# A planner's costs: VectorE and GpSimd use SBUF by turns, ScalarE loads tables, GpSimd's results arrive later

## The chip, the cores and the metric

The kernel runs on one core of a Trainium2 chip. The metric is the device time of one execution in microseconds (us). The engines are named as in the profile: PE (TensorE's products; PEld are its weight loads), DVE (VectorE), ACT (ScalarE), POOL (GpSimd) and SP (SyncE, which here only issues transfers).

## The reference

One layer of a hybrid encoder block on 512 rows of width 1024, in float32. Three sub-layers, each with an RMS norm before and after and a residual sum:

```python
h = rms_norm(x, g_mix_pre)
q_f, k_f, v_f, f_logit, q_c, k_c, v_c = split(h @ w_in)          # 8 + 8 heads of 64
o_f = fox_attention(q_f, k_f, v_f, log_sigmoid(f_logit + b))     # causal, bias c_t - c_s
o_c = chunked_rel_attention(q_c, k_c, v_c, rel_bias)             # chunks of 64, learned bias
mix = concat(rms_norm(o_f), rms_norm(o_c)) @ w_out
x = x + rms_norm(mix, g_mix_post)
x = x + rms_norm(memory_cross_attention(rms_norm(x), rms_norm(mem), w_q, w_kv, w_o))  # 4 heads, 256 tokens
x = x + rms_norm((silu(h @ w_gate) * (h @ w_up)) @ w_down)       # h = rms_norm(x), width 2816
```

## The kernel before

**Products in halves.** Every float32 operand of a large product is split into a rounded half `hi` and a rest `lo`, and the product is made as three PE products: hi by hi, hi by lo and lo by hi (`mm3`, L410, L411, L413). So each block of weights that a transfer brings (`raw`) costs one cast on ACT (`hi`, L392) and one subtraction on DVE (`lo`, L393). That is most of what DVE does.

**Stages.** The first 250 us or so hold the token mixer: four groups of four heads (`order`, first two groups of the forgetting attention, then two of the chunked one). For each group, value, query and key projections (`group_proj`), then the heads. A head (`head`, L787 to L833) walks over four row blocks i = 0 to 3: scores on PE (L796, L797, tile `ps_s`, two banks), sum with the bias and row maximum on DVE (L800, tiles `p_i` and `nm`), exponential on ACT (L810), reciprocal and scaling on DVE (L811, L812), transposes on PE (L815, tile `ps_t`), and the split of the transposed block into `pth` (ACT, L817) and `ptl` (DVE, L818). Then the product with the values (L824, `ps_o`), and ACT and DVE gather the output `o` (L832, L833). After every two heads, `pair_out` writes `oh` (ACT, L836) and `ol` (DVE, L837), and GpSimd squares the output (L843, `o`) and adds it up (L845, `sq`). These sums reach PE in `group_rs` (L851). GpSimd also masks the diagonal block of each bias (L767), adds squares of the memory tokens (L888, `msq`) and raises small tiles to a power for the norms (L418).

The out projection, the memory's keys and values, the queries and the cross-attention follow (softmax rows `xp`, L1067 to L1079; their transposes are split into `pt`, L1085, L1086; products with `vm` into `ps_o`). At the end of the cross-attention a Silu on one column (L1100) makes ACT load the other table of functions ahead of its use. From about 430 us on, the feed-forward stage runs; its order is written out by hand.

**The planner.** Everything up to there is emitted in program order and then put in order by `planned_order` (L90 to L291). It goes through the instructions as a list scheduler: for each engine it keeps the time at which it is free, takes the engine whose next start is earliest, and gives it the ready instruction that comes first in the program (PE prefers to keep its narrow transposes together). `duration` estimates how long an instruction takes; `reached` adds what a result needs to get to another engine (`SIGNAL`, or `TO_PE` for PE); buffers and PSUM banks must be free in its own account (`may_start`). The order so found is then fixed on each engine, PE, DVE, ACT, POOL and SP's queue of transfers alike. So its times don't run the chip; they only decide what stands in front of what.

Of the kernel before, what the change touches and what calls it, by code (L numbers as in the profile page):

```python
# [10 lines left out]
AF = mybir.ActivationFunctionType  # L11
# [24 lines left out]
ENGINES = mybir.EngineType  # L36
MATMUL, NARROW, TURNED, SUMMED, GATHER, ISSUE = 0.4424, 108.0, 12.0, 100.0, 1500.0, 440.0
TAIL = {ENGINES.DVE: 84.0, ENGINES.Activation: 104.0, ENGINES.Pool: 55.0}
SIGNAL = {
    (ENGINES.Activation, ENGINES.DVE): 32.0, (ENGINES.DVE, ENGINES.Activation): 35.0,  # L40
    (ENGINES.PE, ENGINES.Activation): 37.0, (ENGINES.PE, ENGINES.DVE): 37.0,
    (ENGINES.DVE, ENGINES.Pool): 80.0, (ENGINES.Activation, ENGINES.Pool): 67.0,
    (ENGINES.Pool, ENGINES.DVE): 36.0, (ENGINES.Pool, ENGINES.Activation): 34.0,
}
TO_PE, LANDED = 350.0, 60.0


def number(dims):
    n = 1
    for d in dims:  # L50
        n *= d[1]
    return n
# [37 lines left out]
def planned_order(tc, instructions, homes):  # L90


    def tile_of(pattern):
        ap = getattr(pattern, "bass_ap", None)
        return ap.tensor.name if ap is not None and ap.tensor.name in homes.tiles else None

    def in_psum(pattern):
        return homes.tiles[tile_of(pattern)][0] == "ps"
# [24 lines left out]
    def outline(x):  # L123
        return x[:3] + ([(min(a for a, _ in x[3]), max(b for _, b in x[3]))],)

    def duration(i):
        kind = type(i).__name__
        n = number(list(i.outs[0].bass_ap.ap)[1:])
        read = [number(list(a.bass_ap.ap)[1:]) for a in i.ins if tile_of(a)]
        columns = sum(n > 8 and m == 1 for m in read)  # L130
        if i.engine == ENGINES.PE:
            return MATMUL * n + 2.0 if n > P else NARROW
        if i.engine == ENGINES.Activation:
            return (284.0 if len(i.outs) > 1 else 160.0) + 0.838 * n + 80.0 * columns
        if i.engine == ENGINES.Pool:
            if n <= 8:
                return 174.0 if kind == "InstTensorCopy" else 1450.0 if n == 1 else 1040.0
            if kind == "InstTensorTensor" and tile_of(i.ins[0]) != tile_of(i.ins[1]):
                return 25.0 + 4.1 * n
            return 25.0 + (0.96 if kind == "InstMemset" else 2.0) * n  # L140
        if kind == "InstCustomDveAnt":
            return 245.0 + 0.99 * n
        if kind == "InstTensorReduce":
            return 158.0 + 1.02 * read[0]
        if kind == "InstMemset":
            return 70.0 + 0.8 * n
        if kind == "InstReciprocal" or n < 8:
            return 158.0
        full = [a for a in i.ins if tile_of(a) and number(list(a.bass_ap.ap)[1:]) > 8]
        if len(full) < 2 and not any(map(in_psum, full)):  # L150
            return 213.0 + 0.526 * n
        return 150.0 + 1.046 * n + 60.0 * columns

    def halves(i):
        starts = []
        for a in [i.outs[0]] + list(i.ins):
            ap = getattr(a, "bass_ap", None)
            if ap is not None and ap.ap[0][1] >= 8:
                whole = number([(0, n) for n in list(ap.tensor.shape)[1:]]) if tile_of(a) else 0
                starts.append(ap.offset // whole if whole else 0)  # L160
        return (starts + starts + [0, 0])[:2]

    nodes = [i for i in instructions if type(i).__name__ not in ("BassTilePoolBoundary", "InstRegisterMove")]
    written, read, touched, uses, guests, previous, last_of = {}, {}, {}, {}, {}, {}, {}
    after, missing, used = [{} for _ in nodes], [0] * len(nodes), []
    for k, i in enumerate(nodes):
# [14 lines left out]
        for n, x in enumerate(ins + outs):  # L181
            x, writes = outline(x), n >= len(ins) or homes.tiles[x[0]][0] == "ps"
# [19 lines left out]
    for line in after:  # L202
        for k in line:
            missing[k] += 1

    ready, at = {}, [0.0] * len(nodes)
    for k, i in enumerate(nodes):
        if not missing[k]:
            ready.setdefault(i.engine, []).append(k)
    free, ends, place, landed, order, lasts, room = {}, {}, {}, {}, {}, {}, {}  # L210

    def reached(e, other, transfer):
        if e == other and not transfer:
            return 20.0 if e == ENGINES.PE else -20.0
        return TO_PE if other == ENGINES.PE else LANDED if transfer else SIGNAL.get((e, other), 40.0)

    def may_start(k):
        t = at[k]
        for name in used[k]:
            if name in lasts:  # L220
                continue
            if previous[name] and previous[name] not in lasts:
                return None
            key = homes.tiles[name]
            if not room.setdefault(key, [None] * homes.bufs[key]):
                return None
            guest = room[key][0]
            for other in [guest] if guest else [n for n in uses if homes.tiles[n] in homes.under(key)]:
                if uses[other]:
                    return None  # L230
                for (e, transfer), end in lasts[other].items():
                    t = max(t, end + reached(e, nodes[k].engine, transfer))
        return t

    patience = [GATHER if {x for x in names if x in homes.patient} else 0.0 for names in used]
    narrow, after_narrow = [i.engine == ENGINES.PE and duration(i) <= NARROW for i in nodes], False
    while any(ready.values()):
        best = None
        for e, waiting in ready.items():
            starts = [(t, k) for t, k in ((may_start(k), k) for k in waiting) if t is not None]  # L240
            if not starts:
                continue
            now = max(free.get(e, 0.0), min(starts)[0])
            able = [(k, t) for t, k in starts if t <= now + 1.0]
            if e == ENGINES.PE:
                alike = [x for x in able if narrow[x[0]] == after_narrow and (after_narrow or x[1] <= now)]
                late = [x for x in able if narrow[x[0]] and x[1] + patience[x[0]] <= now]
                able = alike if after_narrow and alike else late or alike or able
            if best is None or (now, str(e)) < best[:2]:
                best = now, str(e), e, *min(able)  # L250
        _, _, e, k, t = best
        ready[e].remove(k)
        i, start = nodes[k], max(free.get(e, 0.0), t)
        transfer = type(i).__name__ == "InstDMACopy"
        if transfer:
            free[e] = start + ISSUE
            end = landed[e] = max(start + 1900.0, landed.get(e, 0.0)) + 4 * number(i.outs[0].bass_ap.ap) / 300.0
            if e == ENGINES.Pool:
                end += 1500.0
        elif e == ENGINES.PE:  # L260
            cost = duration(i) + (0.0 if narrow[k] or not after_narrow else SUMMED if summed else TURNED)
            after_narrow, summed = narrow[k], number(list(i.outs[0].bass_ap.ap)[1:]) <= 8
            waited = t > free.get(e, 0.0) + 5.0 and cost > 100.0
            free[e] = start + cost + (95.0 if waited else 0.0)
            end = start + max(cost, 60.0) + 170.0
        else:
            if halves(i) != place.get(e, [0, 0]):
                start = max(start, ends.get(e, 0.0) + 28.0)
            place[e] = halves(i)
            end = ends[e] = start + duration(i)  # L270
            free[e] = max(start + 20.0, end - TAIL[e])
        order.setdefault(e, []).append(i)
        for name in used[k]:
            if name not in lasts:
                lasts[name] = {}
                room[homes.tiles[name]].pop(0)
            lasts[name][e, transfer] = end
            uses[name] -= 1
            if not uses[name]:
                room[homes.tiles[name]].append(name)  # L280
        for j, in_turn in after[k].items():
            other = nodes[j].engine
            at[j] = max(at[j], start if in_turn else (start if e == other == ENGINES.PE else end) + reached(e, other, transfer))
            missing[j] -= 1
            if not missing[j]:
                ready.setdefault(other, []).append(j)
# [15 lines left out]
def hybrid_block_kernel(  # L302
# [628 lines left out]
    with tc.tile_pool(name="cross", bufs=1, reuse_waits="tile") as cp:  # L931
# [508 lines left out]
        class Seven:  # L1440
# [55 lines left out]
        eight(2, gate_eight, IN_STEP)  # L1496
        planned = list(nc.cur_bb.bb.instructions)
        lasts = planned_order(tc, planned, homes)
        own_order = tc.manual_schedule(
            engines={mybir.EngineType.PE, mybir.EngineType.DVE, mybir.EngineType.Activation}  # L1500
# [316 lines left out]
```

## Time and profile before

| | us |
|---|---|
| median of 3 runs (757.09 to 757.48) | 757.11 |
| the profiled execution, whole | 757.56 |
| its span, first to last instruction | 755.8 |
| busy: PE / DVE / ACT / POOL | 744.0 / 603.1 / 445.3 / 59.3 |
| mean granted clock of PE | 0.998 of full |

The profile tells for each instruction its start and length, for each idle stretch what ended it, and from that the chain of waits. Times in it are counted from the start of the span. PE's products are pipelined and their records overlap, so the distance between two starts says more on PE than busy time.

### The profile page before, as it was taken

What the parts mean: (1) busy time and instruction counts of PE and PEld (TensorE: products, weight loads), DVE (VectorE), ACT (ScalarE), POOL (GpSimd) and SP (SyncE); (2) the same over time, 40 slices, a digit from 0 to 9 for tenths busy, and PEclk for the clock granted to TensorE, in tenths of its full rate; (3) what the DMA queues carried; (4) which work ended last, traced back from release to release, by engine and by line L of the source; (5) the groups of instructions that cost most, each with busy time, mean ns of one, the idle gap of its engine ahead of it and who ended that gap; (6) DMA issues with size and microseconds to landing.
All of it is one profiled execution on the core that took longest, in us unless ns stands there. A gap on an engine that the chain in (4) does not pass through costs nothing.

```text
span 755.8 us, 12990 instructions
## 1 busy us (share of the span) xinstructions
PE 744.0 (98%) x5032; PEld 679.8 (90%) x5032; DVE 603.1 (80%) x1101; ACT 445.3 (59%) x817; POOL 59.3 (8%) x101
## 2 busy tenths in 40 slices
PE   9999999999999999999999999999999999999996
PEld 9988887898789988888878999999999999999995
DVE  8669999798788688445654698999989999998756
ACT  8569998686776458344554445666555557544321
POOL 1001232102201211000001200000000000000001
PEclk9999999999999999999999999999999999999999
DMA  7623233324214725411440023333333322243223
GB/s 254 168 81 97 73 88 112 112 71 144 67 57 138 277 75 181 137 57 56 142 145 21 29 97 105 110 110 112 113 112 112 112 85 84 84 139 113 85 84 111
DMA packets 62204, 82.16 MB, mean 109 GB/s; under 512 B 2872, under 2 KB 44344, under 8 KB 62144
## 3 DMA queue, kind: packets, MB, share of 16 engines
q1 hardware_dynamic: 60432, 76.34, 31.8%
q0 software_dynamic: 1280, 4.72, 1.8%
q8 instruction: 39, 0.64, 0.3%
q10 hardware_dynamic: 432, 0.29, 0.1%
q14 instruction: 21, 0.17, 0.1%
HBM read 79.22 MB, written 2.11 MB: 108 GB/s over the span
## 4 chain that ended last, share of the span: by engine, by line
PE 89%; ACT 5%; DVE 3%; issue 1%; DMA 1%; POOL 0%; POOLq 0%; DVEq 0%; ACTq 0%
PE ps_a L410 13%; PE ps_a L411 13%; PE ps_a L413 13%; PE ps_t L1400 3%; PE ps_t L1397 3%; PE ps_t L1398 3%; PE ps_s L1398 3%; PE ps_s L1400 3%; PE ps_s L1397 3%; PE ps_s L410 3%; PE ps_s L413 3%; PE ps_s L411 3%; PE ps_o L824 2%; PE ps_t L815 2%; PE ps_a L1400 1%; PE ps_a L1397 1%
## 5 line engine op out<-in xcount | busy, mean ns | idle before, releaser
L393 DVE TENSOR_TENSOR lo<-raw,hi 128x1024 fp32r<-128x1024 f32 x56 | 69.9, 1258 | 21.1 <-ACT hi L392 13.8
L413 PE MATMUL ps_a<-hTh,lo 128*128 128x512 f32 x192 | 76.2, 397 | 0.0
L411 PE MATMUL ps_a<-hTl,hi 128*128 128x512 f32 x192 | 76.2, 397 | 0.0
L410 PE MATMUL ps_a<-hTh,hi 128*128 128x512 f32 x192 | 75.8, 395 | 0.0
L392 ACT CAST hi<-raw 128x1024 fp32r<-128x1024 f32 x56 | 57.5, 1047 | 30.3 <-PE ps_a L411 20.4
L1193 DVE TENSOR_TENSOR ring_lo<-sums,ring_hi 128x1024 fp32r<-128x1024 f32 (+1 forms) x39 | 46.6, 1195 | 11.8 <-ACT ring_hi L1192 7.2
L1192 ACT CAST ring_hi<-sums 128x1024 fp32r<-128x1024 f32 (+1 forms) x39 | 40.2, 1030 | 16.5 <-PE ps_s L1398 16.5
L1192 ACT CAST ring_hi<-fraw 128x1024 fp32r<-128x1024 f32 (+1 forms) x26 | 26.5, 1032 | 33.6 <-DVE fraw L1279 17.5
L810 ACT ACTIVATE p<-p,nm 128x128 f32<-128x128 f32 (+1 forms) x64 | 36.0, 562 | 11.1 <-DVE nm L800 10.4
L413 PEld LDWEIGHTS ps_a<-hTh,lo 128*128 128x128 f32 x192 | 36.1, 188 | 6.5
L411 PEld LDWEIGHTS ps_a<-hTl,hi 128*128 128x128 f32 x192 | 36.1, 188 | 6.2
L410 PEld LDWEIGHTS ps_a<-hTh,hi 128*128 128x128 f32 x192 | 36.2, 188 | 6.2
L1193 DVE TENSOR_TENSOR ring_lo<-fraw,ring_hi 128x1024 fp32r<-128x1024 f32 (+1 forms) x26 | 30.9, 1199 | 11.3 <-ACT ring_hi L1192 11.3
L818 DVE TENSOR_TENSOR ptl<-ps_t,pth 128x128 fp32r<-128x128 f32 (+1 forms) x64 | 30.4, 483 | 1.7 <-ACT pth L817 1.5
L817 ACT CAST pth<-ps_t 128x128 fp32r<-128x128 f32 (+1 forms) x64 | 26.7, 420 | 8.3 <-PE ps_t L815 7.7
L815 PE MATMUL ps_t<-ident,p 128*128 128x128 f32 x160 | 28.1, 273 | 2.0 <-DVE p L812 2.0
L812 DVE TENSOR_SCALAR p<-p,rc 128x128 f32<-128x128 f32 (+1 forms) x64 | 28.3, 442 | 0.1
L1398 PE MATMUL ps_a<-b,ring_hi 128*128 128x256 f32 x92 | 25.5, 277 | 0.0
L815 PEld LDWEIGHTS ps_t<-ident,p 128*128 128x128 f32 x160 | 19.8, 140 | 6.4 <-issue 1.7
L1397 PE MATMUL ps_a<-b,ring_hi 128*128 128x256 f32 x92 | 25.5, 277 | 0.0
L1400 PE MATMUL ps_a<-b,ring_lo 128*128 128x256 f32 (+1 forms) x93 | 25.5, 276 | 0.0
L410 PE MATMUL ps_a<-hi,oh 128*128 128x512 f32 x64 | 25.3, 396 | 0.0
(572 smaller groups left out, 2774.6 us busy)
## 6 DMA issues: line engine op xcount, KB each, us to landing
raw<-in_dram SPq DMA_DIRECT2D x64, 512.0 KB, 3.7
fraw<-in_dram SPq DMA_DIRECT2D x26, 512.0 KB, 3.5
place<-in_dram SPq DMA_DIRECT2D x21, 512.0 KB, 4.3
more_room<-in_dram SPq DMA_DIRECT2D x15, 512.0 KB, 4.0
row<-gate_rows SPq DMA_DIRECT2D x8, 256.0 KB, 3.2
cb<-in_dram SPq DMA_DIRECT2D x8, 256.0 KB, 2.6
xo<-in_dram POOLq DMA_DIRECT2D x4, 512.0 KB, 7.5
rawv<-in_dram SPq DMA_DIRECT2D x3, 520.0 KB, 6.3
```

The lines of the kernel that those rows point to most:

```text
L392: act.copy(hi[:, j : j + n, :], raw)
L393: dve.tensor_tensor(out=lo[:, j : j + n, :], in0=raw, in1=f32(hi[:, j : j + n, :]), op=ALU.subtract)
L410: pe.matmul(dst, sh, mh, start=first, stop=False)
L411: pe.matmul(dst, sh, ml, start=False, stop=False)
L413: pe.matmul(dst[:, to], sl, mh[:, to], start=False, stop=last)
L810: act.activation(p[:, :n], p[:, :n], AF.Exp, bias=nm, scale=-1.0, accum_out=sm)
L815: pe.transpose(tp[:, k * P : (k + 1) * P], p[:, k * P : (k + 1) * P], ident)
L1192: act.copy(h2, v)
L1193: dve.tensor_tensor(out=l2, in0=v, in1=f32(h2), op=ALU.subtract)
L1397: pe.matmul(dst, w[0][:, k, :], b[:, 0, k, :], start=first and k == 0, stop=False, skip_group_check=more)
L1398: pe.matmul(dst, w[0][:, k, :], b[:, 1, k, :], start=False, stop=False, skip_group_check=more)
L1400: pe.matmul(dst[:, to], w[1][:, k, :], b[:, 0, k, to], start=False, stop=last and k == 3, skip_group_check=more,)
```

## The change

Three things in the planner's account, and nothing else in the kernel:

- DVE and GpSimd instructions of at least 64 columns that read nothing of that size from PSUM (`shares`) are taken to use SBUF by turns. If the other engine still holds it (`port`), the instruction ends later by what is left of that; the hold ends 140 ns (DVE) or 170 ns (POOL) ahead of the instruction's end. With that, GpSimd's sum of two tiles costs 2.46 ns a column, not 4.1.
- If a function of ACT is Exp, Ln or Silu and not the last of these three, the instruction starts 1283 ns later.
- A result is taken to reach PE 900 ns after GpSimd and 400 ns after DVE or ACT, where 350 stood for all.

```diff
-TO_PE, LANDED = 350.0, 60.0
+TO_PE, LANDED = {ENGINES.Pool: 900.0, ENGINES.DVE: 400.0, ENGINES.Activation: 400.0}, 60.0
+TABLES = (AF.Exp, AF.Ln, AF.Silu)
+HOLDS = {ENGINES.DVE: 140.0, ENGINES.Pool: 170.0}
...
             if kind == "InstTensorTensor" and tile_of(i.ins[0]) != tile_of(i.ins[1]):
-                return 25.0 + 4.1 * n
+                return 25.0 + 2.46 * n
...
+    def shares(i):
+        n = number(list(i.outs[0].bass_ap.ap)[1:])
+        return n >= 64 and not any(in_psum(a) for a in i.ins if tile_of(a) and number(list(a.bass_ap.ap)[1:]) >= 64)
+
+    table = [AF.Exp]
+    alone, port = [i.engine in HOLDS and shares(i) for i in nodes], {}
...
-        return TO_PE if other == ENGINES.PE else LANDED if transfer else SIGNAL.get((e, other), 40.0)
+        return TO_PE.get(e, 350.0) if other == ENGINES.PE else LANDED if transfer else SIGNAL.get((e, other), 40.0)
...
             place[e] = halves(i)
+            if getattr(i, "func", None) in TABLES and i.func != table[0]:
+                start, table[0] = start + 1283.0, i.func
             end = ends[e] = start + duration(i)
+            if e in HOLDS and alone[k]:
+                end = ends[e] = end + max(0.0, max(port.get(x, 0.0) for x in HOLDS if x != e) - start)
+                port[e] = end - HOLDS[e]
             free[e] = max(start + 20.0, end - TAIL[e])
```

The instructions stay the same. The order changes on PE, DVE and ACT from the end of the first projections (about 30 us) to the end of the cross-attention, on POOL at four places and on SP at four. Line numbers of the changed kernel are 13 higher from L210 or so on (L406 is L393, L825 is L812, L850 is L837). The prediction speaks of places as follows.

DVE at the second pair of heads. `ol<-o_821` is the pair's output, which GpSimd squares afterwards; `p_1_1216` and `p_2_1232` are row blocks 1 and 2 of the next head, `lo_1583` a weight split. Before:

```order
L837 SCALAR_TENSOR_TENSOR ol<-o_821,gn,oh 128x512
L811 RECIPROCAL rc_1219<-sm_1218 128x1
L800 ISA p_2_1232,nm_1233<-ps_s_1229,fb_2_1189 128x384
L800 ISA nm_1233 128x1
L818 TENSOR_TENSOR ptl_407<-ps_t_1209,pth_406 128x128
L812 TENSOR_SCALAR p_1_1216<-p_1_1216,rc_1219 128x256
L393 TENSOR_TENSOR lo_1583<-raw_0_1584,hi_1582 128x1024
L811 RECIPROCAL rc_1235<-sm_1234 128x1
L818 TENSOR_TENSOR ptl_407<-ps_t_1224,pth_406 128x2x128
L812 TENSOR_SCALAR p_2_1232<-p_2_1232,rc_1235 128x384
```

The same place in the change, on DVE:

```order
L850 SCALAR_TENSOR_TENSOR ol<-o_821,gn,oh 128x512
L831 TENSOR_TENSOR ptl_407<-ps_t_1224,pth_406 128x2x128
L824 RECIPROCAL rc_1235<-sm_1234 128x1
L813 ISA p_3_1249,nm_1250<-ps_s_1246,row_1177 128x512
L813 ISA nm_1250 128x1
L825 TENSOR_SCALAR p_2_1232<-p_2_1232,rc_1235 128x384
L634 SCALAR_TENSOR_TENSOR V_1581<-ps_a_1592,rx_350,V_1581 128x4x64
```

`ol` and the work of GpSimd behind it have moved back past p_1_1216 and the split, and now stand just ahead of the scaling of p_2_1232. On POOL the two masks that stood between and behind L843 and L845 (fb_0_1278, fb_1_1283) now stand ahead of L843.

DVE in the last group. `ol<-o_2478` is again a pair's output, `lo_2996` and `lo_3057` are weight splits, and L800 on p_0_2754 frees the score bank that the scores of p_2_2785 need. Before:

```order
L837 SCALAR_TENSOR_TENSOR ol<-o_2478,gn,oh 128x512
L811 RECIPROCAL rc_2707<-sm_2706 128x1
L800 ISA p_3_2721,nm_2722<-ps_s_2718,cb_2667 128x512
L800 ISA nm_2722 128x1
L818 TENSOR_TENSOR ptl_407<-ps_t_2696,pth_406 128x2x128
L812 TENSOR_SCALAR p_2_2704<-p_2_2704,rc_2707 128x384
L393 TENSOR_TENSOR lo_2996<-raw_4_3001,hi_2995 128x1024
L811 RECIPROCAL rc_2724<-sm_2723 128x1
L800 ISA p_0_2754,nm_2755<-ps_s_2751,cb_2748 128x128
```

And in the change:

```order
L850 SCALAR_TENSOR_TENSOR ol<-o_2478,gn,oh 128x512
L825 TENSOR_SCALAR p_3_2721<-p_3_2721,rc_2724 128x512
L813 ISA p_0_2754,nm_2755<-ps_s_2751,cb_2748 128x128
L813 ISA nm_2755 128x1
L406 TENSOR_TENSOR lo_3057<-raw_0_3058,hi_3056 128x1024
L831 TENSOR_TENSOR ptl_407<-ps_t_2712,pth_406 128x3x128
```

The split that follows `ol` now stands behind the maximum of p_0_2754, not ahead of it.

PE at the end of the cross-attention. `ps_t_4192` are the last transposes of xp, `ps_o_4201` the product that needs both halves of pt; the others are products of the cross-attention's output projection. Before:

```order
L1079 MATMUL ps_t_4192<-ident,xp_4140 128x128 x4
L410 MATMUL ps_a_4324<-woh,oT_3639 128x512
L411 MATMUL ps_a_4324<-wol,oT_3639 128x512
L413 MATMUL ps_a_4324<-woh,oT_3640 128x512
L410 MATMUL ps_a_4324<-woh,oT_3639 128x512
L411 MATMUL ps_a_4324<-wol,oT_3639 128x512
L410 MATMUL ps_o_4201<-pt,vm 128x512
```

And in the change:

```order
L1092 MATMUL ps_t_4192<-ident,xp_4140 128x128 x4
L426 MATMUL ps_a_4298<-hi_4228,oT_3644 128x512
L423 MATMUL ps_a_4298<-hi_4228,oT_3643 128x512
L424 MATMUL ps_a_4298<-lo_4229,oT_3643 128x512
L426 MATMUL ps_a_4298<-hi_4228,oT_3644 128x512
L423 MATMUL ps_a_4324<-woh,oT_3639 128x512
L424 MATMUL ps_a_4324<-wol,oT_3639 128x512
L423 MATMUL ps_o_4201<-pt,vm 128x512
```

Six products now stand between where five stood, and between the transposes of `ps_t_4162`, the first half, and those of ps_t_4192 there are 14 where 7 stood. On ACT, the cast of the first half has moved up by one exponential; the Silu with its table load and one cast of woh stay between the last exponential and the cast of the second half.

On SP, the loads raw_0_1700 and raw_0_2201 now stand ahead of row_1177 and row_1479, the rows of forgetting bias of two heads, and one load and one bias of the chunked heads change places twice more.

## Prediction

> **What bounds the kernel now.** I read the head of the page first, then the busy time by stretches of 25 us, then PE's waits and the timeline of each engine around them. The page, one row for each engine:
>
> ```profile
> span 755.8 us, 12990 instructions
> PE 744.0 (98%) x5032; PEld 679.8 (90%) x5032; DVE 603.1 (80%) x1101; ACT 445.3 (59%) x817; POOL 59.3 (8%) x101
> ```
>
> PE has work for the whole span, so a change of order alone can take away only the time in which PE stands still. The stretches show where the others are nearly as full: columns are the stretch, its length, then the busy us and count of PE, PEld, DVE, ACT, POOL, then PE's granted clock.
>
> ```profile
> 75.00:100.00 25.00, 25.00 (x166) 22.53 (x165) 22.32 (x61) 23.73 (x57) 7.09 (x13) 1.00 0.20 64
> 100.00:125.00 25.00, 23.52 (x144) 20.11 (x143) 23.75 (x68) 21.98 (x55) 7.03 (x15) 1.00 0.45 126
> 575.00:600.00 25.00, 25.00 (x222) 25.00 (x222) 21.63 (x31) 13.97 (x22) 0.00 (x0) 1.00 0.41 127
> ```
>
> The clock is full throughout, so it plays no part. The last row is the feed-forward stage, written out by hand: 222 products of 256 columns in 25 us are 0.113 each, back to back. Nothing is to be had there, and the planner doesn't order it. The second row is attention: PE idle 1.5 us of 25, with DVE busy 23.75. Busy time flatters PE, since records of neighbouring products overlap. So I take the loss of a wait as the distance between two starts, less the usual distance (0.12 behind a product of 256 columns, 0.23 behind one of 512). These are the places where PE lost most outside the start (start, length, engine, line):
>
> ```profile
> 100.83 0.28 PE L413 MATMUL ps_a<-hi,hTl 128*128 128x256 f32 x1
> 101.97 0.30 PE L815 MATMUL ps_t<-ident,p 128*128 128x128 f32 x1 [0.86 <-DVE p L812]
> ...
> 123.73 0.41 PE L824 MATMUL ps_o<-ptl,V 128*128 128x512 f32 x1
> 124.75 0.30 PE L815 MATMUL ps_t<-ident,p 128*128 128x128 f32 x1 [0.62 <-DVE p L812]
> ...
> 140.16 0.39 PE L410 MATMUL ps_a<-hTh,hi 128*128 128x512 f32 x1
> 140.72 0.38 PE L851 MATMUL ps_t<-ones,o 128*128 128x1 f32 x2 [0.16 <-POOL o L843]
> ...
> 199.14 0.28 PE L796 MATMUL ps_s<-T,Q 128*128 128x256 f32 x1
> 199.95 0.44 PE L815 MATMUL ps_t<-ident,p 128*128 128x128 f32 x2 [0.53 <-DVE p L812]
> ...
> 231.04 0.28 PE L411 MATMUL ps_a<-mT,hi 128*128 128x256 f32 x1
> 232.04 0.41 PE L796 MATMUL ps_s<-T,Q 128*128 128x384 f32 x1 [0.72 <-DVE nm L800]
> ...
> 378.65 0.40 PE L411 MATMUL ps_a<-wol,oT 128*128 128x512 f32 x1
> 379.87 0.50 PE L410 MATMUL ps_o<-pt,vm 128*128 128x512 f32 x1 [0.82 <-ACT pt L1085]
> ```
>
> The losses are 1.02 (at 101), 0.79 (124), 0.33 (140), 0.69 (199), 0.89 (231) and 0.99 (378): 4.71 us. That is the whole purse of this change.
>
> Why did PE wait there? For the four on DVE, its row and GpSimd's beside it:
>
> ```profile
> 98.72 1.29 POOL L845 TENSOR_TENSOR sq<-sq,o 128x512 f32<-128x512 f32 x1
> 98.84 2.25 DVE L393 TENSOR_TENSOR lo<-raw,hi 128x1024 fp32r<-128x1024 f32 x1 [0.24 <-ACT hi L392]
> 102.35 1.21 DVE L393 TENSOR_TENSOR lo<-raw,hi 128x1024 fp32r<-128x1024 f32 x1
> ...
> 123.15 1.28 POOL L845 TENSOR_TENSOR sq<-sq,o 128x512 f32<-128x512 f32 x1
> 123.50 1.10 DVE L812 TENSOR_SCALAR p<-p,rc 128x128 f32<-128x128 f32 x1
> ...
> 198.45 1.29 POOL L888 TENSOR_TENSOR msq<-msq 128x512 f32<-128x512 f32 x1 [0.78 <-ACT msq L886]
> 198.43 1.47 DVE L812 TENSOR_SCALAR p<-p,rc 128x256 f32<-128x256 f32 x1
> ...
> 228.14 1.04 POOL L843 TENSOR_TENSOR o<-o 128x512 f32<-128x512 f32 x1 [20.46 <-DVE rc L811]
> 229.26 1.28 POOL L845 TENSOR_TENSOR sq<-sq,o 128x512 f32<-128x512 f32 x1
> 229.32 2.30 DVE L393 TENSOR_TENSOR lo<-raw,hi 128x1024 fp32r<-128x1024 f32 x1
> ```
>
> The weight split L393 takes 1.21 us when alone and 2.25 or 2.30 when it meets GpSimd's L845. The first ends 1.08 after GpSimd's end at 100.01, so it did nearly all its work afterwards: DVE and GpSimd take turns. A short L812, which scales a softmax row, takes 1.10 and 1.47 in the same way. The old planner knows none of this, and PE, whose order is fixed, stands at the transposes L815 or scores L796 behind it. These four losses make 3.39 us. The fifth, at 378, is ScalarE's:
>
> ```profile
> 376.30 0.58 ACT L1085 CAST pt<-ps_t 128x512 fp32r<-128x512 f32 x1
> 376.90 1.28 ACT L1100 ACT_TABLE_LOAD   x1
> 378.19 0.20 ACT L1100 ACTIVATE mix_ms<-xsm 128x1 f32<-128x1 f32 x1
> 378.30 1.03 ACT L392 CAST woh<-raw 128x1024 fp32r<-128x1024 f32 x1
> 379.24 0.58 ACT L1085 CAST pt<-ps_t 128x512 fp32r<-128x512 f32 x1
> ```
>
> The second cast of pt, for which PE waits at 379.87, stands behind a table load of 1.28 us that the old planner takes for nothing.
>
> **The change part by part.** No instruction is added or dropped; costs in the planner change, and with them the order. Its work is PE's work, so each term is a loss that shrinks or a new one. What PE is given to do between a value's origin and its use I call cover, counted in the two orders by size and priced at 0.23, 0.17 and 0.12 us for 512, 384 and 256 columns.
>
> *Turns of DVE and GpSimd* (the ports, and GpSimd's two-tensor cost lowered to 2.46 a column). At 101 the scores and transposes of p_2_1232 have three more products of 256, two of 512 and two of 384 between them: 0.36 + 0.46 + 0.34 = 1.16 of cover against 1.02 lost. But in the new order L843 and L845 together (1.04 + 1.29) follow ol directly and meet the scaling of p_2_1232 itself, so a blocked DVE stays on that path. I take 0.7 gained, with bounds of 0.3 lost and 1.0 gained. At 124 (p_0_1503) cover grows by three products of 512, two of 384 and four of 256: 1.51 against 0.79; 0.7 gained, bounds 0 and 0.8. At 199 (p_1_2500) GpSimd's and DVE's rows around it keep their order, and PE gets three more of 512 and one of 256: 0.81 against 0.69; 0.6 gained. At 231 the score bank was freed by the maximum of p_0_2754, which stood behind the blocked split; now it stands ahead of the split, and seven more products of 256 (0.84) lie before the scores that need the bank; 0.8 of 0.89 gained. Together 2.8.
>
> *The table load.* PE now has 20 products of 512 instead of 12 between the transposes of ps_t_4162 and the product that needs both halves of pt: 8 x 0.23 = 1.84 more against 0.99 lost. ScalarE's order keeps load and woh ahead of the second cast. I take 0.9, bounds 0 and 1.0. The rows show the load starting 0.02 us behind the cast and the next function 0.01 behind the load, so a switch costs 1.28 here. [...]
>
> *Later arrival of GpSimd's results* (900 instead of 350 before PE may use them; 400 for DVE and ScalarE). The sums L851 that wait at 140 now have 47 products of 256 and 6 of 512 ahead of them after the last head's output, 7.0 us, where 22 of 512, 5.1 us, stood. The wait goes; but of the 0.33 lost only 0.16 was idle, and the other 0.17 may be the price of the switch to these narrow products, so I take 0.2 gained, bounds 0 and 0.33. The sums come 1.9 later; what reads them is the eviction of the out projection, which PE only computes during the last group of heads, and loses nothing.
>
> *New losses.* GpSimd's products must all still pass, at other places. I take one new stop of 0.5 (two thirds of the median loss above), bounds 0 and, if three places turn up, 2.4.
>
> Sum: 2.8 + 0.9 + 0.2 - 0.5 = 3.4 us. The profiled execution took 757.56 us (span 755.8 and 1.8 around it) and would take 754.2; it lies 0.45 above the median of the three runs, 757.11, so the forecast is 753.7 us. The cover of all this is the projections of the next head group, of which each head's transposes now have up to 5.5 us more ahead of them, with only 0.5 left of that at the last head: the filler is borrowed, not used up.
>
> **The rivals.** *DVE is the next bound.* DVE was busy 23.75 of 25 at 100:125 and ScalarE 23.73 of 25 at 75:100; a PE that waits less there may just wait at the next row. Then the terms at 101 and 124 (1.4) bring nothing, and of the 3.4 there is 2.0 left: 755.1. Against it: the blocked time itself counts as busy (1.04 at 98.84 alone), and the heads lag the filler.
>
> *The turns fall otherwise than planned.* Who comes first is decided by about 0.1 us (L843 began 0.09 behind the end of ol, 227.31 + 0.74). If the chip's first comer is not the planner's, a whole instruction of 1.0 to 1.3 lands where no cover was laid; the losses move rather than go, and the table load's 0.9 and 0.1 from L851 remain: 756.1.
>
> ```profile
> 227.31 0.74 DVE L837 SCALAR_TENSOR_TENSOR ol<-o,gn,oh 128x512 fp32r<-128x512 f32 x1
> ```
>
> *Slower: the SP queue.* The new order puts the weight load raw_0_1700 ahead of the bias row row_1177, and raw_0_2201 ahead of row_1479. Such a load waits for its buffer, and the row behind it with it. Before, they were issued like this:
>
> ```profile
> 81.36 0.32 SPq L761 DMA_DIRECT2D row<-gate_rows  x1
> 83.06 0.38 SPq L388 DMA_DIRECT2D raw<-in_dram  x1
> ...
> 112.24 0.34 SPq L761 DMA_DIRECT2D row<-gate_rows  x1
> 115.65 0.37 SPq L388 DMA_DIRECT2D raw<-in_dram  x1
> ```
>
> If the loads keep those times, the rows come 1.70 + 0.38 and 3.41 + 0.37 later, 5.9 in all, and with them the first head rows that use them. Where the cover is already spent on GpSimd, PE stands for all of it: 757.1 - 3.4 + 5.9 = 759.6. It decides once the buffer comes free over 1 us later than the row's own. Against it: the splits that free these buffers stand earlier in DVE's new order, and the planner counts the queue.
>
> [...]
>
> **How the numbers follow.** Forecast 0.62; DVE bound 0.13 (755.1, of which 0.10 below and 0.03 above the line of 0.2%); turns otherwise 0.12 (no change); SP queue 0.11 (slower); drain 0.02 (faster). About 0.2%, 1.5 us, is what a measurement of this kernel can tell from no change. Faster: 0.62 + 0.10 + 0.02 = 0.74; same 0.03 + 0.12 = 0.15; slower 0.11. The low end is 757.1 less the whole purse of 4.7 and 0.5 for three unseen stops of 0.17: 751.9. The high end takes in DVE bound and turns otherwise, with 1.5 for two new stops of about 0.75 on top of 756.1: 757.6.
>
> **What would show it.** Right: the idle time of PE on p L812, nm L800 and pt L1085 falls below 1 us in all, blocked L393 and L812 rows are still there, but no PE start behind them is late; PE's starts after 450 us come about 3.4 earlier, with equal distances. The table term is right if the distance ahead of L410's ps_o product (L423 in the changed kernel) is 0.23 to 0.35. The step on DVE is wrong if idle time comes back in 75:135 behind rows that are not blocked; the SP rival shows as ScalarE's L766 waiting for row's DMA. The prediction is wrong if new stops behind blocked rows add up to over 1.5 us.

## The result, and the profile after

The changed kernel takes 752.39 us (median of 4 runs, 751.83 to 752.96) beside 757.30 for the kernel before (4 runs, 757.09 to 757.75): ratio 0.9934, 95% interval 0.9917 to 0.9952. It is faster by 4.9 us, where 3.4 were forecast (753.7, range 751.9 to 757.6). The head of the page after:

```profile
span 750.6 us, 13001 instructions
...
PE 742.4 (99%) x5032; PEld 679.7 (91%) x5032; DVE 602.6 (80%) x1101; ACT 445.2 (59%) x817; POOL 60.3 (8%) x101
```

The span fell by 5.2 us, and every engine has as many instructions as before. One product of the feed-forward stage, the first of its line, before and after, shows where the time was won: columns are start, length, engine and line.

```profile
430.65 0.28 PE L1397 MATMUL ps_a<-b,ring_hi 128*128 128x256 f32 x1
```

```profile
425.43 0.28 PE L1410 MATMUL ps_a<-b,ring_hi 128*128 128x256 f32 x1
```

All 5.2 us are won ahead of that stage, where the planner orders. PE's waits name what went. Before (what PE waited for, us in total, times, longest):

```profile
PE ps_t L815 <- DVE p L812: 2.0, 3, 0.9
PE ps_t L509 <- DVE ones L347: 1.1, 1, 1.1
PE ps_o L410 <- ACT pt L1085: 0.8, 1, 0.8
PE ps_s L796 <- DVE nm L800: 0.7, 1, 0.7
PE ps_t L851 <- POOL o L843: 0.2, 1, 0.2
```

And after (lines 13 higher):

```profile
PE ps_t L522 <- DVE ones L360: 1.1, 1, 1.1
PE ps_t L450 <- DVE hTl L463: 0.2, 1, 0.2
```

The wait for ones is the start of the kernel and stays. The other four lines, 3.7 us of idle time, are gone, and 0.2 came in at another place. The stretch of attention that was short of PE is full now, with DVE as busy as before (23.75):

```profile
100.00:125.00 25.00, 25.00 (x150) 21.69 (x149) 23.95 (x71) 23.02 (x57) 8.52 (x14) 1.00 0.40 115
```

Did DVE and GpSimd stop colliding? Of the four places, two are largely rid of it, one in part and one not at all. At 101 us, where the prediction expected the scaling of p_2_1232 to be blocked, DVE, then GpSimd:

```profile
102.67 0.67 DVE L813 CUSTOM_DVE_ANT_0 p<-ps_s,row 128x512 f32<-128x512 f32 x1
...
103.26 0.42 DVE L825 TENSOR_SCALAR p<-p,rc 128x384 f32<-128x384 f32 x1
```

```profile
102.36 1.04 POOL L856 TENSOR_TENSOR o<-o 128x512 f32<-128x512 f32 x1
103.48 1.35 POOL L858 TENSOR_TENSOR sq<-sq,o 128x512 f32<-128x512 f32 x1
```

GpSimd's square stands beside a row maximum that reads PSUM, and neither is longer than elsewhere (0.67 and 1.04); the scaling behind it takes 0.42, as it does alone. At 228 us, where the split had taken 2.30, it is GpSimd that gives way:

```profile
228.45 1.41 DVE L406 TENSOR_TENSOR lo<-raw,hi 128x1024 fp32r<-128x1024 f32 x1 [0.36 <-ACT hi L405]
```

```profile
228.86 2.17 POOL L858 TENSOR_TENSOR sq<-sq,o 128x512 f32<-128x512 f32 x1
```

Its sum takes 2.17 instead of 1.28, and none of PE's waits names that sum. At 124 us a scaling of 128 columns takes 0.66, where it took 1.10 before and takes 0.28 alone. At 198 us, DVE, then GpSimd, then PE:

```profile
196.03 1.47 DVE L825 TENSOR_SCALAR p<-p,rc 128x256 f32<-128x256 f32 x1
...
198.30 1.32 DVE L825 TENSOR_SCALAR p<-p,rc 128x384 f32<-128x384 f32 x1
...
200.06 0.49 DVE L825 TENSOR_SCALAR p<-p,rc 128x512 f32<-128x512 f32 x1
```

```profile
196.05 1.30 POOL L901 TENSOR_TENSOR msq<-msq 128x512 f32<-128x512 f32 x1 [0.78 <-ACT msq L899]
198.10 1.30 POOL L901 TENSOR_TENSOR msq<-msq 128x512 f32<-128x512 f32 x1 [0.74 <-ACT msq L899]
```

```profile
199.24 0.39 PE L426 MATMUL ps_a<-hi,ol 128*128 128x512 f32 x1
199.76 0.52 PE L828 MATMUL ps_t<-ident,p 128*128 128x128 f32 x3
```

The scaling of 256 columns takes 1.47 us and that of 384 takes 1.32, where the one of 512 alone takes 0.49: both are blocked by GpSimd, as before. I count 11 DVE instructions over 0.15 us longer than the median of their line and shape, against 8 before; together they are 5.98 us too long, against 6.77. So most of the blocking is still there, partly at other places. What is gone is PE's stop behind it: 0.52 from start to start here, 0.29 more than usual behind a product of 512, is the largest left behind such a row.

To compare runs, I sum over all of PE's products the distance from start to start less the usual one (0.4424 ns a column, 0.11 us for 128 columns and fewer; the medians in both profiles are 0.227 us behind 512 columns, 0.108 behind 128 and 0.112 behind one). That loss was 17.85 us before and 12.65 after. By stretches: 75 to 135 us, 3.34 to 1.50; 135 to 150, 0.65 to 0.19; 190 to 210, 1.43 to 0.78; 210 to 250, 1.62 to 0.85; 350 to 400, 2.10 to 0.72. These five make 5.10 of the 5.20. (The first 30 us, the start, hold 3.4 to 4.1 of the loss in any run, so 0.5 us between the totals of two profiles means nothing.)

### The profile page after: what moved, and what is told of

It reads as the page before. It is cut to its first block, busy times and chain, and to the rows that moved or that the text cites. A ratio compares the mean times of both kernels' runs of the same rounds, so it can differ in the third digit from the quotient of the medians.

```text
span 750.6 us, 13001 instructions
## 1 busy us (share of the span) xinstructions
PE 742.4 (99%) x5032; PEld 679.7 (91%) x5032; DVE 602.6 (80%) x1101; ACT 445.2 (59%) x817; POOL 60.3 (8%) x101
## 4 chain that ended last, share of the span: by engine, by line
PE 91%; DVE 4%; ACT 2%; issue 1%; DMA 1%; POOLq 0%; POOL 0%; DVEq 0%; ACTq 0%
PE ps_a L424 14%; PE ps_a L423 14%; PE ps_a L426 14%; PE ps_t L1410 3%; PE ps_t L1413 3%; PE ps_s L1410 3%; PE ps_t L1411 3%; PE ps_s L1411 3%; PE ps_s L1413 3%; PE ps_o L837 3%; PE ps_s L423 3%; PE ps_s L426 3%; PE ps_s L424 3%; PE ps_t L828 2%; PE ps_a L1410 1%; PE ps_a L1413 1%
## 5 line engine op out<-in xcount | busy, mean ns | idle before, releaser
L406 DVE TENSOR_TENSOR lo<-raw,hi 128x1024 fp32r<-128x1024 f32 x56 | 69.4, 1249 | 14.3 <-ACT hi L405 14.1
L825 DVE TENSOR_SCALAR p<-p,rc 128x128 f32<-128x128 f32 (+1 forms) x64 | 28.0, 437 | 0.2
L424 PE MATMUL ps_a<-lo,oh 128*128 128x512 f32 x64 | 25.2, 394 | 0.0
```

Of the source, the lines that this page charges most:

```text
L406: dve.tensor_tensor(out=lo[:, j : j + n, :], in0=raw, in1=f32(hi[:, j : j + n, :]), op=ALU.subtract)
L424: pe.matmul(dst, sh, ml, start=False, stop=False)
```

## The experiments

The theory: PE's losses lie behind collisions and a table load that the old planner took for nothing, and they go when PE's order has cover for them, even where the collisions stay. The rivals: any new order would have been better; or the later arrival at PE, which is slack at every use, is what gave the cover. Each run was timed beside the kernel before on its chip.

| run | this, us | before, us | ratio (95%) | PE's loss, us |
|---|---|---|---|---|
| turns | 753.20 | 757.32 | 0.9951 (0.9938 to 0.9963) | 13.42 |
| table | 755.78 | 757.32 | 0.9982 (0.9973 to 0.9991) | 15.89 |
| arrive | 753.89 | 757.32 | 0.9958 (0.9945 to 0.9970) | 14.46 |
| before_slim | 753.22 | 757.32 | 0.9946 (0.9933 to 0.9958) | 13.53 |
| turns_table | 751.72 | 757.46 | 0.9923 (0.9911 to 0.9936) | 12.01 |
| after_slim | 751.57 | 757.46 | 0.9922 (0.9909 to 0.9934) | 11.87 |
| arrive_rest | 755.55 | 757.46 | 0.9973 (0.9964 to 0.9983) | 16.42 |
| arrive_pool | 757.05 | 757.46 | 0.9995 (0.9986 to 1.0004) | 17.36 |
| before_340 | 759.49 | 757.47 | 1.0028 (1.0017 to 1.0039) | 20.20 |
| before_360 | 756.75 | 757.47 | 0.9991 (0.9983 to 1.0000) | 16.70 |
| turns_table_360 | 752.54 | 757.47 | 0.9936 (0.9923 to 0.9948) | 12.92 |
| turns_table_pool | 751.90 | 757.47 | 0.9926 (0.9913 to 0.9938) | 12.41 |

**Are the collisions the cost? before_slim.** The old order is kept word for word on every engine; only GpSimd's work gets narrow, while the planner still counts 512 columns:

```diff
-                pool.tensor_tensor(out=o, in0=o, in1=o, op=ALU.mult)
+                pool.tensor_tensor(out=o[:, :SLIM], in0=o[:, :SLIM], in1=o[:, :SLIM], op=ALU.mult)
```

and so for the sums into sq and msq, SLIM being 16 (and group_rs keeps its mean of squares at 1 or more).

> The order of the kernel before, instruction for instruction, but GpSimd's squares and sums at L843, L845 and L888 go over 16 columns instead of 512, so that they hold SBUF hardly any more; left out is most of the sums of squares behind the norms. My theory: VectorE's 11 or so blocked rows go, and with them the losses at 101, 124, 199 and 231 us (3.2 to 3.4 us of TensorE's loss), while that at 378 (the table load) stays: about 754.0 (753.6 to 754.6). The rival that the order was unlucky on grounds other than the turns: 757.3, within 0.5.

It took 753.22, 4.1 us less, a little below the expected band. At 99 us, DVE and PE at the place that lost 1.02 before:

```profile
99.09 1.22 DVE L396 TENSOR_TENSOR lo<-raw,hi 128x1024 fp32r<-128x1024 f32 x1 [0.24 <-ACT hi L395]
```

```profile
101.02 0.28 PE L416 MATMUL ps_a<-hi,hTl 128*128 128x256 f32 x1
101.26 0.52 PE L818 MATMUL ps_t<-ident,p 128*128 128x128 f32 x3
```

The split takes 1.22 instead of 2.25, and the transposes follow 0.24 behind the product ahead of them instead of 1.14. PE's waits in this kernel:

```profile
PE ps_t L512 <- DVE ones L350: 1.1, 1, 1.1
PE ps_o L413 <- ACT pt L1088: 0.8, 1, 0.8
```

Behind the start, only the table load's wait is left. So the old order was not bad in itself: without the collisions the stretches around its losses at 101, 124, 140, 199 and 231 us lose 4.1 us less (3.34 to 1.56, 0.65 to 0.23, 1.43 to 0.33, 1.62 to 0.86). At 140 us this run can't tell the collision from GpSimd's own work: there PE waited for the square itself, which took 1.54 us before, beside 1.04 elsewhere, and takes 0.71 with 16 columns.

**The turns alone.** Here the table load and the arrival are taken out of the change:

```diff
-TO_PE, LANDED = {ENGINES.Pool: 900.0, ENGINES.DVE: 400.0, ENGINES.Activation: 400.0}, 60.0
+TO_PE, LANDED = {ENGINES.Pool: 350.0, ENGINES.DVE: 350.0, ENGINES.Activation: 350.0}, 60.0
...
-            if getattr(i, "func", None) in TABLES and i.func != table[0]:
-                start, table[0] = start + 1283.0, i.func
```

> The changed kernel with only the turns left in: the rule of turns, the 2.46 ns a column of VectorE's product, and nothing of the table load or the later arrival. My theory (the losses that go are those behind a blocked VectorE or GpSimd, each term apart): the gain is my four terms of the turns, 2.8 us, so about 754.5 (754.0 to 755.0). The rival that any new order gives the gain, since the old one had bad luck: between 752.5 and 757, without a tie to the 2.8. The rival that the whole gain is the arrival's (a larger distance in time to what TensorE takes): 757.3, no change.

753.20: 4.1 us, not 2.8, and the same as taking the collisions away. That is below the band of my theory and inside the wide one of any new order, which the runs with other distances take up below. The rival that the whole gain is the arrival's is out, since none is in it. The lower cost of GpSimd's sum is part of this run too; put alone into the kernel before, the 2.46 ns leave the order of every engine as it was, so the new order starts from the turns. The same place again, DVE, GpSimd and PE:

```profile
98.54 2.25 DVE L404 TENSOR_TENSOR lo<-raw,hi 128x1024 fp32r<-128x1024 f32 x1 [0.25 <-ACT hi L403]
...
101.71 0.41 DVE L823 TENSOR_SCALAR p<-p,rc 128x384 f32<-128x384 f32 x1
```

```profile
98.42 1.28 POOL L856 TENSOR_TENSOR sq<-sq,o 128x512 f32<-128x512 f32 x1
```

```profile
102.28 0.29 PE L421 MATMUL ps_a<-hi,hTh 128*128 128x256 f32 x1
102.41 0.49 PE L826 MATMUL ps_t<-ident,p 128*128 128x128 f32 x3
```

The collision is as long as before, 2.25 us beside GpSimd's 1.28. Here the planner doesn't avoid it, it books it: its DVE comes free later (on the chip by 2.25 less 1.22, some 1.0), so it gives PE other products first, and the transposes start 0.13 behind the product ahead of them. In this kernel, too, PE's only wait behind the start is the one for pt, 0.8.

**The table load alone.** Of the change only this is left:

```diff
+TABLES = (AF.Exp, AF.Ln, AF.Silu)
...
+    table = [AF.Exp]
...
+            if getattr(i, "func", None) in TABLES and i.func != table[0]:
+                start, table[0] = start + 1283.0, i.func
```

> The changed kernel with only the 1283 ns of ScalarE's table load left in. My theory: only the loss of 0.99 us at 378 us goes, by my term 0.9 us of it, so about 756.4 (756.2 to 756.6). The rival that any new order gives the gain: this order is the nearest to that of before, so up to 1 us either way. The rival of the arrival: 757.3, no change.

755.78: 1.5 us less, 0.6 more than expected and below the band. ScalarE at the end of the cross-attention in this run:

```profile
375.97 0.58 ACT L1095 CAST pt<-ps_t 128x512 fp32r<-128x512 f32 x1
376.57 1.28 ACT L1110 ACT_TABLE_LOAD   x1
377.87 0.20 ACT L1110 ACTIVATE mix_ms<-xsm 128x1 f32<-128x1 f32 x1
377.98 0.57 ACT L1095 CAST pt<-ps_t 128x512 fp32r<-128x512 f32 x1
378.44 1.05 ACT L402 CAST woh<-raw 128x1024 fp32r<-128x1024 f32 x1
```

Before, the cast of woh (1.03) stood between the load and the second cast of pt; a planner that knows of the load's 1.28 us puts pt first. The loss at 378 (0.99) is gone, and so is one of 0.31 that the kernel before had at 389.57 and that I had not put in the purse. The other five places keep their losses. The load still starts 0.02 after the cast, and the function follows 0.02 after it.

**The arrival alone.** Of the change only this is left:

```diff
-TO_PE, LANDED = 350.0, 60.0
+TO_PE, LANDED = {ENGINES.Pool: 900.0, ENGINES.DVE: 400.0, ENGINES.Activation: 400.0}, 60.0
...
-        return TO_PE if other == ENGINES.PE else LANDED if transfer else SIGNAL.get((e, other), 40.0)
+        return TO_PE.get(e, 350.0) if other == ENGINES.PE else LANDED if transfer else SIGNAL.get((e, other), 40.0)
```

> The changed kernel with only the later arrival at TensorE left in (900 ns for GpSimd's results, 400 for the others'). My theory: 0.2 us, so about 757.1 (756.6 to 757.3); what the changed kernel gained over my 3.4 us could be this part's margin, then down to 755.8 (1.5 us more). The rival that the arrival's margin is what covers all the waits: 753 to 754. The rival that any new order gives the gain: 752.5 to 757.

753.89: 3.4 us, the rival's figure, against 0.2 by my step. So the distance alone can take away most of the waits. It does so largely by moving collisions: in this trace no split near 99 or 230 us takes over 1.32, where two took 2.25 and 2.30 before. Which part of it? Two halves, GpSimd's 900 alone, and 400 alone for the other two:

```diff
-TO_PE, LANDED = 350.0, 60.0
+TO_PE, LANDED = {ENGINES.Pool: 900.0, ENGINES.DVE: 350.0, ENGINES.Activation: 350.0}, 60.0
```

```diff
-TO_PE, LANDED = 350.0, 60.0
+TO_PE, LANDED = {ENGINES.Pool: 350.0, ENGINES.DVE: 400.0, ENGINES.Activation: 400.0}, 60.0
```

> The kernel before with 900 ns instead of 350 to TensorE for GpSimd's results alone. By my step, the loss of 0.33 us at 140 us goes and no other: 757.0 (756.7 to 757.3). If GpSimd's margin is what the 3.4 us of the whole arrival came from: 754.

> The kernel before with 400 ns instead of 350 to TensorE for the results of VectorE and ScalarE, and 350 for GpSimd's as before. The whole arrival alone took 3.4 us off where my step said 0.2. If the 50 ns are what did it: 754 or so. If GpSimd's 900 did it: 757. My theory of the turns gives neither a figure by itself: 50 ns are too little to cover a wait of 0.7 to 1.0 us, so this is the new order's own luck, and could be anything from 753 to 758.

GpSimd's 900 gives 0.4 (no sure difference), and the stretch 135 to 150 falls from 0.65 to 0.16: my step, at its size. The 50 ns give 1.9, although they cannot cover a wait of 1 us. The profiled run of arrive_rest holds something more. After PE waited for GpSimd's squares, the clock was halved (PE's rows, then stretches with the granted clock behind the busy times):

```profile
142.67 0.28 PE L419 MATMUL ps_a<-lo,hTh 128*128 128x256 f32 x1
143.33 0.38 PE L859 MATMUL ps_t<-ones,o 128*128 128x1 f32 x2 [0.38 <-POOL o L851]
...
144.69 0.36 PE L859 MATMUL ps_t<-ones,o 128*128 128x1 f32 x2
```

```profile
145.00:146.00 1.00, 1.00 (x10) 1.00 (x10) 0.88 (x5) 0.26 (x1) 0.46 (x1) 1.00 0.38 132
146.00:147.00 1.00, 1.00 (x6) 1.00 (x6) 1.00 (x3) 0.23 (x2) 0.56 (x1) 0.51 0.00 0
...
148.00:149.00 1.00, 1.00 (x6) 1.00 (x6) 0.81 (x4) 0.00 (x0) 0.00 (x0) 0.50 0.88 332
149.00:149.50 0.50, 0.50 (x5) 0.50 (x4) 0.00 (x0) 0.00 (x0) 0.00 (x0) 0.57 0.81 311
```

From 146.0 to about 149.4 us PE ran at half clock, and half of 3.4 us, 1.7, is lost. Its ten runs fall in two groups of five, 754.39 to 755.11 and 755.98 to 756.65, with medians 1.7 apart; their mean granted clock is 0.997 to 0.999 in the first and 0.995 to 0.997 in the second. One run was traced, so the halved clock is read for the others from these two figures. Without it the 50 ns would be worth 2.8 (757.46 less 754.63, the median of the lower five). In arrive, where GpSimd's 900 puts the sums later, PE doesn't stop there (busy 12.00 us of 12 from 138 to 150 us) and keeps its clock (1.00 in that stretch).

**Is it the luck of an order?** Two runs of the kernel before with 340 and 360 ns for all engines, a change that pays for nothing by itself:

```diff
-TO_PE, LANDED = 350.0, 60.0
+TO_PE, LANDED = 340.0, 60.0
```

> The kernel before with 340 ns instead of 350 to TensorE, which no theory can pay for by itself: it only has the planner choose another order (394 rows of TensorE's differ). It asks how much of the 3.4 us of the later arrival is the luck of an order. If orders without the turns scatter by the losses they happen to keep: between 754 and 759. If the order of before was an unlucky one, 753.5 to 755. If the time follows the distance of time, 757.3 to 757.8.

> The same with 360 ns (352 rows of TensorE's differ from before). Scatter: between 754 and 759. An unlucky order before: 753.5 to 755. A time that follows the distance: 757.3, since 400 ns for two engines gave 755.55.

759.49, a little above the band for scatter, and 756.75, at the edge of what its interval can tell from no change. PE's waits with 340:

```profile
PE ps_t L815 <- DVE p L812: 1.9, 3, 0.9
PE ps_s L796 <- DVE nm L800: 1.5, 2, 0.7
...
PE ps_a L410 <- ACT oT L1095: 0.7, 1, 0.7
PE ps_a L410 <- ACT y L1137: 0.6, 1, 0.6
```

A planner that is 10 ns off moves the time by 2.0 us up or 0.7 down. Without the turns and the load, the orders tried give 753.9 to 759.5, by the waits that they happen to keep: with 340 PE loses 2.07 more than before from 75 to 135 us, where three blocked rows of DVE stand (at 81, 101 and 126 us), but also 0.78 more from 350 to 400, where the waits for oT and y stand. With 340, 350, 360 and 400 (DVE and ScalarE alone, without the halved clock) the times fall in that order; whether that is a trend or four draws these runs don't tell.

**The turns and the table load together,** with 350 ns as before. The edit, from the changed kernel:

```diff
-TO_PE, LANDED = {ENGINES.Pool: 900.0, ENGINES.DVE: 400.0, ENGINES.Activation: 400.0}, 60.0
+TO_PE, LANDED = {ENGINES.Pool: 350.0, ENGINES.DVE: 350.0, ENGINES.Activation: 350.0}, 60.0
```

> The changed kernel without the later arrival (350 ns for every engine, as before), with the turns and the table load. My theory (turns and table load add up, the arrival is spare): 4.1 and 1.5 us from the two runs apart, so about 751.7, or, where the sum is cut by what the changed kernel still loses, 752.0 to 752.5. The rival that the changed kernel needs the arrival's margin: 753.2 or more, the time of the turns alone.

751.72, as the sum of the two (4.1 + 1.5) had it, and 0.7 below the changed kernel's median; the ranges of the runs (751.45 to 751.76, and 751.83 to 752.96) don't overlap, though the intervals of the ratios do. Its waits:

```profile
PE ps_t L522 <- DVE ones L360: 1.1, 1, 1.1
PE ps_s L423 <- DVE vhi L568: 0.3, 1, 0.3
```

So the arrival is not needed. Two more orders under the same two rules, 360 ns for all, and GpSimd's 900 with 350 for the rest:

```diff
+TO_PE, LANDED = {ENGINES.Pool: 360.0, ENGINES.DVE: 360.0, ENGINES.Activation: 360.0}, 60.0
...
+        return TO_PE.get(e, 360.0) if other == ENGINES.PE else LANDED if transfer else SIGNAL.get((e, other), 40.0)
```

```diff
+TO_PE, LANDED = {ENGINES.Pool: 900.0, ENGINES.DVE: 350.0, ENGINES.Activation: 350.0}, 60.0
```

> The turns and the table load with 360 ns to TensorE for every engine instead of 350 (370 rows of TensorE's differ from the run of turns and table load). If the two rules put right what cost the time, another order under them is as good: 751.7, within 0.6. If the 751.7 was a lucky order: 753 to 756.

> The changed kernel with 350 ns to TensorE for VectorE and ScalarE, and GpSimd's 900 kept. It tells which half of the arrival costs the changed kernel the 0.7 us by which the run without any arrival is faster, and it could be the fastest. If the 50 ns of the two engines: 751.7. If GpSimd's 900: 752.4.

752.54, at 0.8 a little outside the 0.6 that I allowed, and 751.90. Four orders with both rules, the changed kernel's among them, lie between 751.7 and 752.5, where seven without the turns (the kernel before, table, and the five with another distance alone) lie between 753.9 and 759.5. The best of the seven, arrive, is only 0.7 above the turns alone, so a lucky order can gain nearly as much as that rule; what sets the two rules apart is that all four orders tried under both are good. The last run puts the 0.7 on the 50 ns of DVE and ScalarE rather than on GpSimd's 900, but 360 ns for all costs as much, so it is within what any reordering does here.

**What is left of the collisions: after_slim.** The changed kernel's order, with GpSimd's work narrowed by the same edit as in before_slim (the planner still counts it at 512 columns and among the turns):

```diff
-                    pool.tensor_tensor(out=sq, in0=sq, in1=o, op=ALU.add)
+                    pool.tensor_tensor(out=sq[:, :SLIM], in0=sq[:, :SLIM], in1=o[:, :SLIM], op=ALU.add)
```

> The order of the changed kernel, instruction for instruction, with GpSimd's squares and sums at L856, L858 and L901 over 16 columns instead of 512 (left out is most of the sums of squares behind the norms). My theory: the changed order has the blocked rows under cover, so that taking them away gives at most the 0.3 us still lost at 199 us: 752.0 to 752.5. The rival that blocked rows still cost the changed kernel in many small pieces: 751 or less.

751.57, 0.8 less, between the two theories. The loss at 190 to 210 us falls from 0.78 to 0.37, which is the one stop that I named; at 250 to 350 from 1.35 to 0.87, where the wait for hTl is gone. So what cost 4.1 us in the old order costs about 0.8 in the new one.

## Why the prediction was right, and where its sizes were off

The mechanism held in the main: PE has the same products, and it stopped standing behind DVE, GpSimd and the table load. What did not hold is the picture that all blocked rows stay. Term by term, by the stretches of the changed kernel:

- **Turns, 2.8.** 3.26 came at the three stretches, 4.1 in the run of the turns alone. The mis-sized step is the one at 101 and 124 us: 1.84 came where I had 1.4. At 101 I left 0.3 in place because "a blocked DVE stays on that path". That reading failed: in the changed kernel the scaling of p_2_1232 takes 0.42 and isn't blocked; GpSimd's square (1.04) runs beside a row that reads PSUM (0.67), and neither is longer than elsewhere. At 231 the size was right (0.8, and 0.77 came), but the split is hardly blocked either: it takes 1.41, where it took 2.30. At 199 both hold: the blocked rows stay, and 0.65 came where I had 0.6. In the run of the turns alone the stop at 140, which I gave to the arrival, goes too: the stretch 135 to 150 falls from 0.65 to 0.24 without any arrival.
- **Table load, 0.9.** In the changed kernel 0.22 of the 0.99 is left:

```profile
374.02 0.40 PE L424 MATMUL ps_a<-wol,oT 128*128 128x512 f32 x1
374.46 0.50 PE L423 MATMUL ps_o<-pt,vm 128*128 128x512 f32 x1
```

  0.44 from start to start, where I had said 0.23 to 0.35, so by my own sign this term falls short at its place: 0.77 came. But the 0.31 at 389.57, outside my purse, went too; the stretch 350 to 400 gave 1.38, and the load alone 1.5. A planner that counts 1283 ns puts the cast right. Among the prediction's chances stand 0.02 for a drain at the switch of tables, which no run shows: in the kernel before, the changed one and the run of the table load alone, the rows show a load of 1.28 us with 0.02 us or less on both sides of it.
- **Arrival, 0.2.** By GpSimd's half alone 0.4, unsure, at the place named. Put on top of the other two parts, it brought nothing (751.72 without, 752.39 with). Alone, the whole arrival gives 3.4, by another order, most of which the 50 ns of the other engines bring (2.8 without the halved clock). My step didn't look at them, and why so little time does so much stays open.
- **New losses, -0.5.** New stops came at about this size, 0.39 at 290 (transposes waiting for hTl) and 0.20 at 430. But others went that I hadn't counted, and the stretch 250 to 350 as a whole lost what it lost before (1.37 and 1.35), so the term is nothing net. This step, which left out what a new order takes away unseen, failed.

So all four terms were off the same way: 3.26 for 2.8, 1.38 for 0.9, 0.46 for 0.2 (the stretch 135 to 150), and nothing for -0.5. No error made up for another.

The gains of the three parts run alone don't add up to the change: 4.1 + 1.5 + 3.4 is 9.0. They take away the same stops.

The rivals: DVE as the next bound is out, with PE at 25.00 of 25 while DVE has 23.95. Turns that fall otherwise than planned: whoever came first, the losses didn't move, since the stretches around all four places lose less. The SP queue: its sign was ScalarE's waiting for a row of bias. Before, ScalarE's waits have this line (us in total, times, longest); after, they have none of its kind:

```profile
ACT fb L766 <- DMA row<-gate_rows: 1.5, 2, 1.3
```

The expectation that PE would idle less than 1 us in all on p, nm and pt held (none listed), and PE's starts after 450 us came 5.2 earlier, not 3.4.

## What to carry to other kernels

Where a planner fixes each queue's order, a contention that it doesn't know costs at the engine that waits (here PE; before_slim, nearly without the contention, is 4.1 us faster), not at the two that collide: let it book the longer time at the right place, and the wait can go though the collision stays (the split of 2.25 us in the run of the turns), or the collision falls where nobody waits for it. Test such a cost by taking the contention away in an unchanged order, and test a new order against some that differ by a few nanoseconds in a constant, since here 10 ns either way gave 756.8 and 759.5 us. A part that gains alone may add nothing behind the others, so the last of three rules needs its own run with the other two in place.

## What the runs showed of the hardware

In arrive_rest PE's granted clock was 0.50 to 0.51 from 146.0 to about 149.4 us, 3.4 us in all, and 1.00 in the stretches before and behind. Behind a product of 256 columns the distance from start to start was 0.21 us then, where it is 0.12 otherwise. It began 2.7 us after the end of a stop with 0.38 us of idle time, behind which PE made only one-column products from 143.33 to 144.91. The longer stops of the kernel before (0.86 us of idle time at 101, 0.82 at 378) were not followed by it: from 100 to 125 and from 375 to 400 us its granted clock is 1.00. So in these two traces the length of a stop alone doesn't tell whether the clock is halved. What does, these runs don't show; of the ten runs of arrive_rest only one was traced.

The blocking of DVE and GpSimd is mutual: beside the collisions that stretch DVE's rows, GpSimd's own are stretched by the splits, a mask of 0.29 us to 1.28:

```profile
99.67 1.28 POOL L778 TENSOR_SCALAR_AFFINE_SELECT fb<-fb 128x128 f32<-128x128 f32 x1
```

```profile
98.03 0.29 POOL L770 TENSOR_SCALAR_AFFINE_SELECT fb<-fb 128x128 f32<-128x128 f32 x1 [0.23 <-ACT fb L769]
```

The first row, in the run of the turns alone, stands beside the split of 98.54 to 100.79, of whose 2.25 us 1.09 lie behind the end of GpSimd's sum at 99.70; the second is one in before_slim with no split beside it.
